# A planner that orders a hybrid trunk's work: a longer visit of small work, and key transposes that come with those of the first queries

## The chip, the cores and the metric

The kernel runs on one core of one Trainium2 chip. The metric is the device time of one execution in microseconds (us). Of the kernel before there are three timed runs, and one further execution under the hardware profiler, from which all rows of the profile come.

## The reference

The reference is a decoder trunk of two residual layers for one sequence of 256 tokens and 1024 channels, in float32. Each layer norms its input, projects it with one wide matrix, feeds three causal mixers in parallel, projects each of them, merges them by sigmoid gates, and projects once more:

```
for layer in range(2):
    h = rms_norm(x, norm_w[layer])
    (a_xbc, a_z, a_dt, b_q, b_k, b_v, b_z, c_q, c_k, c_v, c_f, c_z, gates) = split(h @ w_in[layer])
    y_a = mamba2_branch(a_xbc, a_z, a_dt, ...)           # conv of 4 taps, SiLU, SSD scan, gate, grouped norm
    y_b = sliding_window_branch(b_q, b_k, b_v, b_z, sinks[layer], cos, sin)
    y_c = forgetting_attention_branch(c_q, c_k, c_v, c_f, c_z, ...)
    branch = einsum('bsiw,iwd->bsid', stack(y_a, y_b, y_c), w_proj[layer])
    merged = sum(sigmoid(gates + gate_bias[layer]) * branch)
    x = x + merged @ w_out[layer]
return rms_norm(x, final_norm_w)
```

The sliding branch is what the change is about. It has 16 query heads and 4 key heads of 64 channels. Queries and keys are turned by the rope; each block of 128 queries sees its own and the preceding block of 128 keys under a band mask; a sink per head takes part in the softmax; the result is multiplied by SiLU of b_z.

## The kernel before

**Dense work.** All projections are matmuls in fp32r with weights and inputs split into a high and a low part (hi, lo), in three passes: hi·hi, lo·hi, hi·lo. One dense op is 24 matmuls of 256 or 512 columns into one of three PSUM banks (tiles called mm). A weight tile comes raw from memory (load_to, L368, on SP's queue, which handles its DMAs strictly in order; 6 raw buffers), and ScalarE makes hi (L289) and VectorE lo (L290), 6 buffers each. A unit function (u_bkv, u_bq, u_conv, u_z, u_cv and so on) issues one dense op, then what empties its bank, and then calls pump(). Ops of 512 columns also call it in their middle.

**Small work.** Transposes, scores, softmax, values and the SSD groups are generators that put themselves on a list called waiting by launch(branch, generator, delay), and again with the delay that they yield. A clock that the planner keeps for itself advances with every TensorE instruction that is written out. pump() enters the generator that has been due longest, if one is due and its condition holds, and goes on to the next as long as this visit has used less than BUDGET of the planner's clock:

```
def pump(budget=BUDGET):
    t0 = clock["t"]
    while clock["t"] - t0 < budget:
        for m in sorted(waiting, key=lambda m: (m[0], m[1])):
            if ready(m):
                enter(m)
                break
        else:
            return
```

TensorE runs precisely in this written order. The order on VectorE, ScalarE, GpSimd and SP behind the start is set by a scheduler from the same program, each engine then taking its instructions in order.

**Sliding keys.** u_bkv computes keys and values of one token block (t = 0 or 1), turns the keys by the rope (POOL adds the parts at L529) and launches rest with the delay D_K. rest transposes the keys (L101, to PSUM tiles mx), copies them to kT (L540, ScalarE), and for t = 1, four clock units later, issues two DMAs on SP (L544, 64 partitions each) that write each half of kT to the other half of the partitions. Only then may the scores start.

**Sliding queries.** u_bq does the same with the queries; its rest has the delay D_Q = 5.5, copies at L566 to a tile qt, and for t = 1 launches swa_quad for four heads. swa_quad has three visits to TensorE: 16 scores of a 64-row key tile against qt (mm by L97 into mx); then, behind the softmax (VectorE L671, L674, L681, L684, L686 and L689; ScalarE exp L678 and L683), 8 transposes of pp, which ScalarE copies (L701, L702) and POOL masks (L703, L705); then 16 values, whose product with the gate VectorE takes (L720). A token named pp lets only one quad at a time be between its scores and its values. There are four quads in a layer.

**Between the quads** run the convolutions of the SSD branch: u_conv empties its bank with L799 and L800 on ScalarE, applies three taps on VectorE (L803), a tanh on ScalarE (L806) and a product (L807); u_z makes gates (L863, L866); u_cv makes values of the third branch. The cumulative sums go through memory (cumd: L786 out, L818 and L941 back, on ScalarE's queue). Constants such as the norm's vector (vr, L284) also come on ScalarE's queue.

Of the kernel before, what the change touches and what calls it, by code (L numbers as in the profile page):

```python
# [22 lines left out]
EPS = 1e-6  # L23

D_SOFT, D_EVAC, D_SSD, D_SSD2 = 9.0, 3.0, 8.0, 3.0
D_K, D_Q, D_QK, D_G0, D_FOX, D_BDMA, D_BIAS = 6.0, 5.5, 2.0, 8.0, 0.0, 4.0, 2.0
D_SEL, D_CONST, D_NWB = 5.0, 1.5, 10.0
D_GN1, D_GN2, D_CUM, D_H, D_M = 6.5, 2.5, 12.0, (4.8, 7.0), 5.0
BUDGET = 1.35
T_PP, T_SSD, T_BIAS = 1, 1, 1  # L30
N_RAW, N_SPLIT = 6, 6
AHEAD = 4
# [12 lines left out]
def hybrid_trunk(  # L45
# [83 lines left out]
# [10 lines that stand above are left out]
# [1235 lines left out]
```

## Time and profile before

| what | value |
|---|---|
| three timed runs | 827.72, 828.05, 830.84 us (median 828.05) |
| the profiled execution | 828.2 us, of which the span of all recorded instructions is 826.5 us |
| granted TensorE clock, mean | 0.997 |
| DMA | 158.39 MB, mean 192 GB/s over the span |
| layer 0's sliding quads, conv and SSD | about 50 to 131 us of the span |
| the same of layer 1 | about 455 to 536 us |

PE is TensorE, PEld its loading of weights, DVE VectorE, ACT ScalarE, POOL GpSimd, SP the engine that issues most DMAs. An instruction's row in the timeline has its start, its duration, engine, line, operation, output and inputs by the program's names, and the count when like rows are put together (then the duration goes from the first start to the last end). Matmuls overlap, so starts tell more than durations. In square brackets stands how long the engine was idle before, and what ended that.

### The profile page before, as it was taken

What the parts mean: (1) busy time and instruction counts of PE and PEld (TensorE: products, weight loads), DVE (VectorE), ACT (ScalarE), POOL (GpSimd) and SP (SyncE); (2) the same over time, 40 slices, a digit from 0 to 9 for tenths busy, and PEclk for the clock granted to TensorE, in tenths of its full rate; (3) what the DMA queues carried; (4) which work ended last, traced back from release to release, by engine and by line L of the source; (5) the groups of instructions that cost most, each with busy time, mean ns of one, the idle gap of its engine ahead of it and who ended that gap; (6) DMA issues with size and microseconds to landing.
All of it is one profiled execution on the core that took longest, in us unless ns stands there. A gap on an engine that the chain in (4) does not pass through costs nothing.

```text
span 826.5 us, 15576 instructions
## 1 busy us (share of the span) xinstructions
PE 816.6 (99%) x5777; PEld 743.7 (90%) x5777; DVE 653.8 (79%) x1333; ACT 499.2 (60%) x974; POOL 91.6 (11%) x151
## 2 busy tenths in 40 slices
PE   8999999999999999999999999999999999999996
PEld 7899898988999998888999988898899999988896
DVE  7787998999666788875786879989986667878665
ACT  6476687646666675543664757775556667645442
POOL 3210301000111102100014011100001110021000
PEclk9999999999999999999999999999999999999998
DMA  8945555665765656775687464456676665576632
GB/s 293 287 148 172 178 179 192 181 213 184 213 173 157 215 177 192 225 230 182 213 262 235 135 221 140 138 186 206 190 240 180 178 180 167 162 232 218 217 105 74
DMA packets 124174, 158.39 MB, mean 192 GB/s; under 512 B 12850, under 2 KB 85026, under 8 KB 124099
## 3 DMA queue, kind: packets, MB, share of 16 engines
q1 hardware_dynamic: 109888, 140.92, 55.9%
q10 hardware_dynamic: 14162, 16.36, 6.5%
q8 instruction: 45, 0.74, 0.4%
q14 instruction: 31, 0.25, 0.1%
q0 software_dynamic: 48, 0.13, 0.0%
HBM read 154.70 MB, written 2.16 MB: 190 GB/s over the span
## 4 chain that ended last, share of the span: by engine, by line
PE 94%; DVE 2%; DMA 1%; issue 1%; ACT 1%; ACTq 0%; POOLq 0%; POOL 0%
PE mm L97 79%; PE mx L97 11%; PE mx L101 4%; DMA cumd<-L 1%; DVE lo L290 1%; DVE pp L671 1%; DVE pp L689 0%; DVE L L803 0%; DVE pp L674 0%; ACT L L800 0%; DVE L L866 0%; ACT L L784 0%; ACT L L863 0%; ACT L L799 0%; ACTq L818 0%
## 5 line engine op out<-in xcount | busy, mean ns | idle before, releaser
L290 DVE TENSOR_TENSOR lo<-raw,hi 128x1024 fp32r<-128x1024 f32 x252 | 307.2, 1232 | 64.1 <-ACT hi L289 61.2
L97 PE MATMUL mm<-hi,L 128*128 128x512 f32 (+1 forms) x1264 | 347.7, 363 | 0.9 <-ACT L L800 0.9
L97 PE MATMUL mm<-L,hi 128*128 128x256 f32 x1792 | 310.4, 277 | 0.0
L289 ACT ACTIVATE hi<-raw 128x1024 fp32r<-128x1024 f32 x252 | 261.1, 1054 | 68.7 <-PE mm L97 66.6
L97 PEld LDWEIGHTS mm<-L,hi 128*128 128x128 f32 x1792 | 275.4, 192 | 5.2 <-issue 3.7
L97 PEld LDWEIGHTS mm<-hi,L 128*128 128x128 f32 x1264 | 226.4, 189 | 29.8 <-issue 2.5
L97 PE MATMUL mm<-L,lo 128*128 128x256 f32 x896 | 246.4, 275 | 0.0
L97 PE MATMUL mm<-lo,L 128*128 128x512 f32 (+1 forms) x632 | 224.4, 360 | 0.0
L97 PEld LDWEIGHTS mm<-L,lo 128*128 128x128 f32 x896 | 172.0, 192 | 0.2
L97 PEld LDWEIGHTS mm<-lo,L 128*128 128x128 f32 x632 | 118.8, 189 | 13.7
L948 POOL TENSOR_SCALAR_AFFINE_SELECT bias<-bias 128x128 f32<-128x128 f32 x64 | 24.7, 419 | 290.3 <-DMA bias<-cumd 290.3
L803 DVE SCALAR_TENSOR_TENSOR L<-L,vec,L 128x255 f32<-128x255 f32 (+2 forms) x96 | 47.1, 491 | 4.4 <-ACT L L800 3.1
L972 ACT ACTIVATE L<-L 128x512 f32<-128x512 f32 x24 | 15.1, 630 | 43.0 <-DVE L L971 43.0
L806 ACT ACTIVATE L<-L 128x256 f32<-128x256 f32 x32 | 13.5, 421 | 45.3 <-DVE L L803 45.3
L605 ACT ACTIVATE pp<-pp,nm 128x128 f32<-128x128 f32 x64 | 28.2, 445 | 14.2 <-DVE nm L599 14.2
L97 PE MATMUL mx<-L,L 128*64 128x128 f32 (+1 forms) x384 | 36.5, 332 | 0.0
L97 PEld LDWEIGHTS mx<-L,L 128*64 128x64 f32 x384 | 23.8, 136 | 11.7 <-issue 1.7
L678 ACT ACTIVATE pp<-pp,nm 128x128 f32<-128x128 f32 x64 | 25.3, 395 | 11.7 <-DVE nm L671 6.6
L863 ACT ACTIVATE L<-mm 128x256 f32<-128x256 f32 x48 | 18.1, 376 | 23.0 <-PE mm L97 22.7
L671 DVE CUSTOM_DVE_ANT_0 pp<-mx,wmask,nsink 128x128 f32<-128x128 f32 x64 | 24.3, 412 | 6.0 <-PE mx L97 6.0
L866 DVE SCALAR_TENSOR_TENSOR L<-L,mm 128x256 f32<-128x256 f32 x32 | 13.3, 416 | 16.2 <-ACT L L863 16.2
L97 PE MATMUL mx<-hi,L 128*128 128x512 f32 (+1 forms) x80 | 21.7, 363 | 0.3 <-ACT L L1270 0.2
(184 smaller groups left out, 783.4 us busy)
## 6 DMA issues: line engine op xcount, KB each, us to landing
raw<-in_w_in_dram SPq DMA_DIRECT2D x200, 512.0 KB, 4.6
raw<-in_w_proj_dram SPq DMA_DIRECT2D x48, 512.0 KB, 4.8
raw<-in_w_out_dram SPq DMA_DIRECT2D x16, 512.0 KB, 4.6
L<-cumd ACTq DMA_DIRECT2D x8, 512.0 KB, 3.6
bias<-cumd ACTq DMA_DIRECT2D x16, 256.0 KB, 3.8
L<-in_gate_bias_dram ACTq DMA_DIRECT2D x12, 256.0 KB, 4.2
L<-in_x_dram SPq DMA_DIRECT2D x2, 512.0 KB, 4.0
out_dram<-L SPq DMA_DIRECT2D x2, 320.0 KB, 2.5
```

Source lines behind the costliest of these rows:

```text
L97: nc.tensor.matmul(o, a, b, **kw)
L101: nc.tensor.transpose(o, a, i)
L289: keep(act)(hi, src, AF.Copy)
L290: keep(tt)(lo, src, hi.bitcast(F32), op=ALU.subtract)
L605: act(pp[:, i, sl], pp[:, i, sl], AF.Exp, scale=-1.0, bias=nm[:, e:e + 1], accum_out=sums[:, e:e + 1])
L671: nc.vector.tensor_tensor_reduce(out=pp[:, i, sl], in0=score(p, i, b), in1=m, scale=-0.125, scalar=ns[:, i:i + 1], op0=ALU.add, op1=ALU.mi ...
L678: act(pp[:, i, sl], pp[:, i, sl], AF.Exp, scale=-1.0, bias=nm[:, e:e + 1], accum_out=sums[:, e:e + 1])
L803: stt(a[:, s:S], x_[:, 0:S - s], y.vec[:, 16 * j + u:16 * j + u + 1], a[:, s:S], op0=ALU.mult, op1=ALU.add)
L806: act(th, a, AF.Tanh)
L863: act(halves(th), p, AF.Tanh, scale=0.5)
L948: nc.gpsimd.affine_select(out=bias[:, i, dst], in_=bias[:, i, src], compare_op=ALU.is_ge, fill=NEG, base=0, pattern=[[-1, P]], channel_mul ...
L972: act(g, g, AF.Tanh, scale=0.5)
```

## The change

Two numbers of the planner are changed, and nothing else:

```
-D_K, D_Q, D_QK, D_G0, D_FOX, D_BDMA, D_BIAS = 6.0, 5.5, 2.0, 8.0, 0.0, 4.0, 2.0
+D_K, D_Q, D_QK, D_G0, D_FOX, D_BDMA, D_BIAS = 14.0, 5.5, 2.0, 8.0, 0.0, 4.0, 2.0
...
-BUDGET = 1.35
+BUDGET = 2.0
```

With D_K the keys' transposes are due 14 clock units after the rope instead of 6. With BUDGET a visit that has used 1.35 to 2.0 units may still enter another generator. The number of instructions stays the same on each engine. What the two do to the order shows at three places.

On TensorE, layer 0, where the first sliding quad's values end (mx_1033 is their output, L_56_289 holds kT and the values, qt the second quad's queries, mm_1043 and mm_1093 are the same dense op of u_z, 24 matmuls; numbers of tiles shift between the programs):

```order
 L97 MATMUL mx_1033<-L_202_948,L_56_289 64x256 x2
 L97 MATMUL mx_1033<-L_198_932,L_56_289 64x128 x2
-L97 MATMUL mm_1043<-L_24_147,hi_877 128x256
-L97 MATMUL mm_1043<-L_24_147,lo_878 128x256
-L97 MATMUL mm_1043<-L_25_148,hi_877 128x256
...
+L97 MATMUL mx_1047<-L_56_289,qt_421 128x128
+L97 MATMUL mx_1048<-L_56_289,qt_421 128x128
...
+L97 MATMUL mm_1093<-L_24_147,hi_877 128x256
+L97 MATMUL mm_1093<-L_24_147,lo_878 128x256
+L97 MATMUL mm_1093<-L_25_148,hi_877 128x256
```

The second quad's scores follow the values directly, and the dense op that stood between comes behind them. Layer 1 has the same at the same place. From there to about the fourth quad the small visits of the quads come one dense op, or half of one of 512 columns, earlier than before.

On ScalarE, layer 0, the rows behind the second quad's exponentials, before:

```order
L678 ACTIVATE pp_1084,sums_1086<-pp_1084,nm_1085 128x128 x3
L799 ACTIVATE L_241_1160<-mm_1133 128x256
L678 ACTIVATE pp_1084,sums_1086<-pp_1084,nm_1085 128x128
L683 ACTIVATE es_1126<-es_1126 128x4
L800 ACTIVATE L_240_1159<-mm_1133,vec_647 128x256
L289 ACTIVATE hi_1264<-raw_970 128x1024
L289 ACTIVATE hi_1282<-raw_988 128x1024
```

and now, of the same engine from the same exponentials on:

```order
L678 ACTIVATE pp_1044,sums_1046<-pp_1044,nm_1045 128x128 x4
L683 ACTIVATE es_1086<-es_1086 128x4
L863 ACTIVATE L_237_1130<-mm_1093 128x256
L289 ACTIVATE hi_1182<-raw_881 128x1024
L289 ACTIVATE hi_1200<-raw_899 128x1024
L818 DMA L_439_2214<-cumd_1031 128x1024
L799 ACTIVATE L_241_1160<-mm_1133 128x256
L800 ACTIVATE L_240_1159<-mm_1133,vec_647 128x256
```

The exponentials of the second quad (pp) have moved ahead of the first convolution's bank copies (mm_1133, L799 and L800), and no longer mix with them.

On SP, layer 0, the weight loads and the two DMAs of kT (L544; one row stands for both):

```order
-L368 DMA raw_451<-in_w_in_dram 128x4x256
-L368 DMA raw_463<-in_w_in_dram 128x4x256
-L544 DMA L_56_289<-L_56_289 64x2x256 x2
+L368 DMA raw_441<-in_w_in_dram 128x4x256
+L368 DMA raw_453<-in_w_in_dram 128x4x256
+L368 DMA raw_466<-in_w_in_dram 128x4x256
 L368 DMA raw_478<-in_w_in_dram 128x4x256
-L368 DMA raw_490<-in_w_in_dram 128x4x256
 L368 DMA raw_576<-in_w_in_dram 128x4x256
 L368 DMA raw_582<-in_w_in_dram 128x4x256
+L544 DMA L_56_289<-L_56_289 64x2x256 x2
```

The kT DMAs stand behind four more weight loads than before (raw_478, raw_490, raw_576 and raw_582 by the names before); in layer 1 they also stand behind four more. The keys' transposes on TensorE come, for layer 0, in one visit with the first queries', and for the second token block of layer 1 with queries of the same block, one dense op behind where those stood.

## The prediction

> **What bounds the kernel now.** I read the page first, then the list of TensorE's waits, then the two places where that list says time is lost, then the queues that the change moves. From the page:
>
> ```profile
> span 826.5 us, 15576 instructions
> PE 816.6 (99%) x5777; PEld 743.7 (90%) x5777; DVE 653.8 (79%) x1333; ACT 499.2 (60%) x974; POOL 91.6 (11%) x151
> PEclk9999999999999999999999999999999999999998
> PE 94%; DVE 2%; DMA 1%; issue 1%; ACT 1%; ACTq 0%; POOLq 0%; POOL 0%
> ```
>
> TensorE is busy for 99% of the span, at a full granted clock, and 94% of the chain that ends last is its work. So a change of order can only move time in two ways: it takes away or adds a wait of TensorE, or it changes what TensorE pays between two kinds of matmul. All waits that the view of TensorE's waits lists (total, times, longest, in us):
>
> ```profile
> PE mx L101 <- POOL ident masks.py:199: 1.5, 1, 1.5
> PE mm L97 <- ACT L L800: 0.9, 2, 0.5
> PE mx L97 <- ACT L L1270: 0.2, 1, 0.2
> PE mx L101 <- issue: 0.2, 1, 0.2
> ```
>
> The first is the start of the kernel, which the change leaves alone. Behind it 1.3 us are left, and 0.9 of these are two waits for one thing, a copy by ScalarE at L800. They are the only ones within the stretches that the change orders anew. Since no more than that is there to be won, a gain of over 4 us has no place to come from. The measurement of this kernel can tell about 0.5% (4 us) from no change.
>
> The timeline of TensorE shows these two waits (start, duration, x count). The first two rows are a visit of the same kind that does not wait; the next two are layer 0's, the last two layer 1's:
>
> ```profile
> 107.86 1.04 PE L101 MATMUL mx<-ident,pp 128*128 128x128 f32 x8
> 108.66 0.36 PE L97 MATMUL mm<-L,hi 128*128 128x256 f32 x1
> ...
> 87.39 1.04 PE L101 MATMUL mx<-ident,pp 128*128 128x128 f32 x8
> 88.88 0.70 PE L97 MATMUL mm<-hi,L 128*128 128x512 f32 x2 [0.45 <-ACT L L800]
> ...
> 492.21 1.04 PE L101 MATMUL mx<-ident,pp 128*128 128x128 f32 x8
> 493.74 0.70 PE L97 MATMUL mm<-hi,L 128*128 128x512 f32 x2 [0.49 <-ACT L L800]
> ```
>
> Undisturbed, eight transposes take 0.80 us from their first start to the next dense matmul (107.86 to 108.66). Here it is 1.49 and 1.53: 0.69 + 0.73 = 1.42 us lost. (The bracket says 0.45 and 0.49, because a busy matmul's end is modelled; I go by starts.) The cause stands in ScalarE's and VectorE's timelines of layer 0:
>
> ```profile
> 83.45 1.05 ACT L289 ACTIVATE hi<-raw 128x1024 fp32r<-128x1024 f32 x1
> 87.69 0.42 ACT L806 ACTIVATE L<-L 128x256 f32<-128x256 f32 x1 [3.18 <-DVE L L803]
> 88.01 0.36 ACT L799 ACTIVATE L<-mm 128x256 f32<-128x256 f32 x1
> 88.27 0.56 ACT L800 ACTIVATE L<-mm,vec 128x256 f32<-128x256 f32 x1
> ...
> 84.98 0.69 DVE L689 TENSOR_TENSOR pp<-pp,rsum 128x512 f32<-128x512 f32 x1
> 87.11 0.48 DVE L803 SCALAR_TENSOR_TENSOR L<-L,vec,L 128x253 f32<-128x253 f32 x1
> ```
>
> ScalarE stands 3.18 us in front of the tanh of one convolution (L806). That waits for the last tap on VectorE (L803, 87.11), which stood behind the softmax of the second quad (L689, 84.98). Behind the tanh in ScalarE's queue are L799 and L800 of the next convolution, which empty a PSUM bank; TensorE's next op in that bank starts 0.05 us after L800's 0.56 us are over (88.27 + 0.56 = 88.83; 88.88).
>
> **The change part by part.** *The visit that lasts longer.* In each layer, at one place, the scores of the second quad now follow the values of the first; before, one dense op of 24 matmuls of 256 columns stood between. The matmuls are the same, so what is saved is what TensorE pays between kinds. The rows of the separate visits, and of one visit that was merged already:
>
> ```profile
> 71.22 1.04 PE L97 MATMUL mx<-L,L 128*64 128x128 f32 x12
> 72.19 0.38 PE L97 MATMUL mm<-L,hi 128*128 128x256 f32 x1
> 72.40 0.28 PE L97 MATMUL mm<-L,lo 128*128 128x256 f32 x1
> 72.51 0.28 PE L97 MATMUL mm<-L,hi 128*128 128x256 f32 x1
> ...
> 74.86 0.28 PE L97 MATMUL mm<-L,hi 128*128 128x256 f32 x1
> 75.06 0.93 PE L97 MATMUL mx<-L,qt 64*128 64x128 f32 x8
> ...
> 94.74 1.04 PE L97 MATMUL mx<-L,L 128*64 128x128 f32 x12
> 95.71 0.93 PE L97 MATMUL mx<-L,qt 64*128 64x128 f32 x8
> ```
>
> Twelve values take 0.97 us to the start of what follows, be it dense work (71.22 to 72.19) or scores (94.74 to 95.71). But the first dense matmul then holds its successor for 0.21 (72.19 to 72.40) where 0.11 is the rule (72.40 to 72.51), and the last one before scores takes 0.20 (74.86 to 75.06). Merged, both extras go: 0.10 + 0.09 = 0.19 us a place, two places, **−0.4 us**. [...]
>
> *What follows from it.* The softmax of the second quad starts one dense op (24 x 0.11 = 2.7 us) earlier, and its transposes come earlier too. On ScalarE its exponentials now stand ahead of L799/L800 of the first convolutions instead of among them, and on VectorE its last product (84.98) comes about 2.7 us earlier, at 82.3, ahead of the taps. Then the tap of 87.11 is over near 84.9, tanh and the next convolution's L799/L800 by 86.2 (0.42 + 0.36 + 0.56), and TensorE wants the bank at 88.0 (87.39 + 0.80 less the 0.2 of the merged visit): 1.8 us to spare. **−1.4 us** for the two stalls. What is late next: the values of the same quad wait for GpSimd's mask of the exponentials' transposes, as they do now:
>
> ```profile
> 94.11 0.58 POOL L705 TENSOR_SCALAR_AFFINE_SELECT L<-L 128x256 f32<-128x256 f32 x1
> ```
>
> The mask ends at 94.69, 0.05 us ahead of values at 94.74. Everything in that chain of visits moves by the same step, so I take no new wait; if ScalarE's copies ahead of the mask are late by as much as an L289 (1.05 us in the rows above), each layer loses up to 1.0 us.
>
> *The keys' transposes.* The same transposes, copies (L540) and DMAs (L544) come later. A visit of transposes costs TensorE no extra beyond the 0.08 us of one slow successor (108.66's row), so merging with the queries' saves at most 0.1 us a time: 0. What can cost is the landing of the L544 DMAs ahead of the first scores. Layer 1, where it is tightest; the timeline rows of TensorE, ScalarE and SP, and the source view of L544:
>
> ```profile
> 443.67 0.60 PE L101 MATMUL mx<-ident,L 128*128 128x128 f32 x4
> 454.84 0.93 PE L97 MATMUL mx<-L,qt 64*128 64x128 f32 x8
> ...
> 438.46 0.78 ACT L540 ACTIVATE L<-mx 64x256 f32<-64x256 f32 x2 [4.40 <-PE mx L101]
> 438.87 1.29 SPq L544 DMA_DIRECT2D L<-L  x2
> 446.56 0.37 SPq L368 DMA_DIRECT2D raw<-in_w_in_dram  x1
> 450.80 0.37 SPq L368 DMA_DIRECT2D raw<-in_w_in_dram  x1
> ...
> DMA to landing us min/median/max: 2.7/5.0/7.4
> ```
>
> In the new order the transposes stand one dense op behind the place at 443.67, about 446.3. Six transposes (0.7) and two pairs of copies (2 x 0.78) bring it to about 448.4. The DMAs stand on SP behind four more weight loads, of which the last issued at 446.56 before, so SP is free: issues at 448.4 and 449.0. Landing at 451.7 by the shortest row, 454.0 by the median, 456.4 by the longest, against scores at 454.84. I take the short one, since both layer-1 rows are of this place: 3 us to spare, **0 us**; the far end is +1.6 us. Behind them on SP waits the load of 450.80, which isn't reached. In layer 0 the DMAs go from 27.2 to about 36, and the scores start at 50: 36 + 7.4 leaves 6 us.
>
> One DMA that the diff does not name moves with them. In layer 0 the load of the norm's vector on ScalarE's queue now waits for the landing of a weight that SP issues near 32.2:
>
> ```profile
> 32.23 2.92 SPq L368 DMA_DIRECT2D raw<-in_w_in_dram  x3
> ...
> 45.42 0.24 PE L101 MATMUL mx<-ident,vr 88*128 88x88 f32 x1
> ...
> DMA to landing us min/median/max: 3.1/5.4/12.2
> ```
>
> With 7.4 us for that weight (the longest L544 above, issued in the same stretch) it issues at 39.6, and with its own line's median of 5.4 (last row) lands at 45.0, against its transpose at 45.42. I take +0.1 us; with the longest, 12.2, it would be +6.4.
>
> **The sum** is made against the profiled execution, 828.2 us (span 826.5 and 1.7 around it), 0.15 above the median of the three runs shown (828.05). 828.2 − 0.4 − 1.4 + 0 + 0.1 = 826.5. Set against the median it is 826.3; I say 826.4.
>
> **The rivals.** *The stalls change place.* Another of the engines' queues holds the bank, or the mask is late: −0.4 remains and about as much is lost elsewhere (1.4 us, up to 2.0 with the mask in both layers): 827.8 to 828.4. For it: a bank goes back only 0.05 us ahead of its use today, and masks likewise. Against: by the starts above there are 1.8 us in hand. 0.20.
>
> *Slower: the key copies are late in layer 1.* The last weight load in front of them comes free one step later, at 450.80 and not 446.56; then they issue at 451.2 and 451.8 and land at 454.5, 456.8 or 459.2. It decides from a landing after 454.84: 0, +2.0 or +4.4 us, with a gain of 1.7 beside it: 826.5 to 830.9, likeliest 828.5 where it bites. For it: the buffers of raw weights set those times, and the order of their readers shifts. Against: nothing else was moved there. 0.08. The clock: the PEclk row is full throughout, and no wait of TensorE in it exceeds 1.5 us. [...] 0.01.
>
> *Slower: the norm vector is late in layer 0.* It decides from a landing time of 5.8 us (45.42 − 39.6), close to the median of 5.4; at 12.2 it costs 6.4: 826.4 to 832.8. For it: four weight loads are in flight at that time. Against: few rows are that long. 0.08.
>
> **How the numbers follow.** Forecast 0.57 (826.4; by its bounds 825.6 to 828), stalls elsewhere 0.20, keys late 0.08, clock 0.01, norm vector 0.08, a wait that I don't see in the reordered stretch 0.05 (up to 8 us), a gain that I don't see 0.01. Faster by over 0.5% (under 823.9) only by the last: 0.02 with the spread of runs. Slower by over 0.5% (over 832.2): the unseen wait, the upper end of the norm vector and the clock, 0.05 + 0.02 + 0.01 = 0.08. The rest, 0.90, is within. The range goes from 825.5 to 830.9, the upper end of the keys' case.
>
> **What would show it.** Right: no row with a wait for L800 near 86 to 89 and 490 to 494; the second quad's scores right behind the first's values, near 72 us; all waits behind the start under 0.6 us in sum. Wrong: a wait of the 64*128 scores for a DMA near 455, of the 88x88 transpose for a DMA near 45, of values for L705, or again for L800. A span 4 us away from 825 would mean that a wait was missed, or that TensorE's busy time is not the same for the same matmuls.

## The result and the profile after

The changed kernel takes 836.83 us (median of 6 runs, 834.47 to 838.27); the kernel before, over the runs taken beside it and earlier, 829.2 us (827.26 to 830.84). The ratio is 1.0094, with a 95% interval of 1.0079 to 1.011: slower by 0.9%, where 0.2% faster was forecast. The profiled execution takes 836.13 us, with a span of 834.0. Its page:

```profile
span 834.0 us, 15592 instructions
PE 820.0 (98%) x5777; PEld 745.7 (89%) x5777; DVE 654.7 (78%) x1333; ACT 500.5 (60%) x974; POOL 92.1 (11%) x151
...
PEclk9999899999999999999999999999999999999999
...
PE 91%; issue 6%; POOL 2%; ACT 0%; DVE 0%; POOLq 0%
```

The work is the same; the chain now has POOL in it, and the clock row has an 8 in its fifth slice. (The 6% of issue are two pieces of 22 us, one in each layer, in which the chain runs through POOL's idle time ahead of L948.) The view of TensorE's waits (total, times, longest):

```profile
PE mx L97 <- POOL L L703: 3.1, 3, 1.3
PE mx L97 <- POOL L L705: 2.3, 3, 1.2
PE mx L101 <- POOL ident masks.py:199: 1.5, 1, 1.5
PE mm L97 <- ACT L L1270: 0.2, 1, 0.2
```

The two waits for L800 are gone, as forecast. In their place stand 5.4 us of waits for the masks of the second sliding quad. POOL's timeline of layer 0, the kernel before:

```profile
87.18 1.53 POOL L948 TENSOR_SCALAR_AFFINE_SELECT bias<-bias 128x128 f32<-128x128 f32 x4 [20.84 <-DMA bias<-cumd]
89.35 2.38 POOL L948 TENSOR_SCALAR_AFFINE_SELECT bias<-bias 128x128 f32<-128x128 f32 x4 [0.64 <-DMA bias<-cumd]
91.69 1.38 POOL L703 TENSOR_SCALAR_AFFINE_SELECT L<-L 128x256 f32<-128x256 f32 x1
```

and the changed one:

```profile
88.64 2.77 POOL L948 TENSOR_SCALAR_AFFINE_SELECT bias<-bias 128x128 f32<-128x128 f32 x4 [22.44 <-DMA bias<-cumd]
91.36 0.58 POOL L703 TENSOR_SCALAR_AFFINE_SELECT L<-L 128x256 f32<-128x256 f32 x1
91.90 1.39 POOL L705 TENSOR_SCALAR_AFFINE_SELECT L<-L 128x256 f32<-128x256 f32 x1
93.24 0.58 POOL L703 TENSOR_SCALAR_AFFINE_SELECT L<-L 128x256 f32<-128x256 f32 x1
93.78 1.22 POOL L948 TENSOR_SCALAR_AFFINE_SELECT bias<-bias 128x128 f32<-128x128 f32 x4
94.97 0.41 POOL L705 TENSOR_SCALAR_AFFINE_SELECT L<-L 128x256 f32<-128x256 f32 x1
```

L948 makes the causal masks of the third branch's bias tiles, which are read back from memory (L941). They belong to work much later, but POOL takes them in its queue's order when they land. Before, both tiles stood ahead of the quad's masks. Now the transposes come 3 us earlier (84.38 instead of 87.39), the first tile still stands ahead of the masks, and the second tile stands between the third mask and the fourth. TensorE's timeline shows what that costs; first the changed kernel's layer 0, then its layer 1:

```profile
90.31 0.38 PE L97 MATMUL mm<-lo,L 128*128 128x512 f32 x1
92.00 0.65 PE L97 MATMUL mx<-L,L 128*64 128x256 f32 x4 [1.31 <-POOL L L703]
93.34 1.66 PE L97 MATMUL mx<-L,L 128*64 128x128 f32 x8 [0.69 <-POOL L L705]
95.42 0.69 PE L97 MATMUL mx<-L,L 128*64 128x128 f32 x4 [0.42 <-POOL L L705]
96.05 2.93 PE L97 MATMUL mx<-L,qt 64*128 64x128 f32 x16
98.91 1.22 PE L97 MATMUL mm<-hi,L 128*128 128x512 f32 x2
...
500.17 0.38 PE L97 MATMUL mm<-lo,L 128*128 128x512 f32 x1
...
505.54 1.58 PE L97 MATMUL mx<-L,qt 64*128 64x128 f32 x16
507.05 0.70 PE L97 MATMUL mm<-hi,L 128*128 128x512 f32 x2
```

From the last dense matmul to the next one it takes 8.60 us in layer 0 and 6.88 in layer 1. The same visit without a wait takes 3.28 (it is in the run a_late below, 93.12 to 96.40). So 5.3 and 3.6 us are lost. In layer 0 part of this is the clock, because TensorE runs at half speed there (granted clock 0.50 from 94 to 100 us): from the first score to the next dense matmul it takes 2.86 us (96.05 to 98.91) instead of the 1.51 of a_late (94.89 to 96.40). Behind the visit another 0.6 us go the same way: the next five dense matmuls take 1.80 us (98.91 to 100.71) instead of the 1.18 of layer 1 (507.05 to 508.23). The windows view has the granted clock as the number behind POOL's busy time and count:

```profile
90.00:92.00 2.00, 0.69 (x4) 0.26 (x3) 2.00 (x4) 1.67 (x4) 2.00 (x4) 1.00 0.15 54
92.00:94.00 2.00, 1.31 (x10) 0.61 (x12) 1.97 (x3) 0.00 (x0) 2.00 (x3) 0.84 0.80 217
94.00:96.00 2.00, 1.58 (x10) 0.47 (x8) 0.10 (x1) 0.00 (x0) 1.37 (x5) 0.50 0.87 261
96.00:98.00 2.00, 2.00 (x16) 1.78 (x16) 1.35 (x3) 0.42 (x1) 0.00 (x0) 0.50 0.13 50
98.00:100.00 2.00, 2.00 (x9) 1.17 (x8) 2.00 (x13) 1.38 (x6) 0.00 (x0) 0.50 0.01 4
100.00:102.00 2.00, 2.00 (x10) 1.77 (x9) 2.00 (x13) 1.83 (x9) 0.00 (x0) 0.95 0.00 0
```

The account closes: 5.3 + 0.6 + 3.6 lost, 1.4 (L800) and 0.4 (the merged visits) won, 7.7 in all; from the first dense matmul to the end the two profiles differ by 819.97 − 812.35 = 7.6 us.

### The profile page after: what moved, and what is told of

The parts are those of the page before. It is cut to its first block, busy times and chain, and to the rows that moved or that the text cites. A ratio compares the mean times of both kernels' runs of the same rounds, so it can differ in the third digit from the quotient of the medians.

```text
span 834.0 us, 15592 instructions
## 1 busy us (share of the span) xinstructions
PE 820.0 (98%) x5777; PEld 745.7 (89%) x5777; DVE 654.7 (78%) x1333; ACT 500.5 (60%) x974; POOL 92.1 (11%) x151
## 4 chain that ended last, share of the span: by engine, by line
PE 91%; issue 6%; POOL 2%; ACT 0%; DVE 0%; POOLq 0%
PE mm L97 77%; PE mx L97 10%; PE mx L101 4%; POOL bias L948 1%; POOL L L703 1%; POOL L L705 0%; ACT L L701 0%; ACT L L1110 0%; ACT L L1270 0%; POOLq L1370 0%; ACT L L226 0%; DVE L L1090 0%; POOL ident masks.py:199 0%; POOLq L948 0%; DVE sm L239 0%
## 5 line engine op out<-in xcount | busy, mean ns | idle before, releaser
L290 DVE TENSOR_TENSOR lo<-raw,hi 128x1024 fp32r<-128x1024 f32 x252 | 307.8, 1234 | 67.4 <-ACT hi L289 61.9
L289 ACT ACTIVATE hi<-raw 128x1024 fp32r<-128x1024 f32 x252 | 261.7, 1054 | 61.2 <-PE mm L97 58.5
L948 POOL TENSOR_SCALAR_AFFINE_SELECT bias<-bias 128x128 f32<-128x128 f32 x64 | 25.1, 425 | 300.7 <-DMA bias<-cumd 172.3
L97 PE MATMUL mx<-L,L 128*64 128x128 f32 (+1 forms) x384 | 38.5, 340 | 5.4 <-POOL L L703 3.1
```

Of the source, the lines that this page charges most:

```text
L97: nc.tensor.matmul(o, a, b, **kw)
L289: keep(act)(hi, src, AF.Copy)
L290: keep(tt)(lo, src, hi.bitcast(F32), op=ALU.subtract)
L948: nc.gpsimd.affine_select(out=bias[:, i, dst], in_=bias[:, i, src], compare_op=ALU.is_ge, fill=NEG, base=0, pattern=[[-1, P]], channel_mul ...
```

## The experiments

**How they are compared.** The start of the kernel takes one of two lengths, and the times of the kernel before fall into two groups 2.5 to 3 us apart. TensorE's timelines show it at the first dense matmul, here of before (828.2 us) and of dk_only (830.82 us):

```profile
14.15 0.75 PE L97 MATMUL mm<-hi,L 128*128 128x256 f32 x4
...
16.94 0.73 PE L97 MATMUL mm<-hi,L 128*128 128x256 f32 x4 [0.22 <-ACT L L1270]
```

For a single profile the table therefore also has the time from there to the span's end, in which the start does not count. It is one execution each, and the span is read to 0.1 us; the ratios with their intervals come from the timed runs, each against runs of before taken beside it. The medians of those were 829.2 for changed, 828.53 for dk_only, budget_only, a_late and b_late, 828.81 for a_late2, warm and a_late_soft, and 830.43 for a_dma and a_dma_soft, so ratios compare and medians do not.

| kernel | median us (runs) | ratio to before (95%) | first dense matmul to end, us |
|---|---|---|---|
| before | see above | 1 | 812.35 |
| changed | 836.83 (6) | 1.0094 (1.0079 to 1.011) | 819.97 |
| dk_only | 828.27 (10) | 0.9997 (0.9982 to 1.0011) | 812.16 |
| budget_only | 835.89 (4) | 1.0082 (1.0061 to 1.0104) | 819.76 |
| b_late | 830.3 (12) | 1.0007 (0.9993 to 1.0022) | 812.33 |
| a_late | 828.9 (12) | 0.9995 (0.998 to 1.0009) | 811.56 |
| a_late2 | 830.1 (10) | 1.0015 (0.9999 to 1.0031) | 811.37 |
| warm | 836.17 (4) | 1.0081 (1.0062 to 1.01) | 817.91 |
| a_dma | 830.52 (10) | 1.002 (1.0005 to 1.0035) | 814.26 |
| a_dma_soft | 830.17 (12) | 1.0021 (1.0007 to 1.0034) | 814.28 |
| a_late_soft | 826.31 (12) | 0.9971 (0.9958 to 0.9983) | 810.46 |

**dk_only and budget_only: which of the two numbers.** `D_K = 14.0` alone, and `BUDGET = 2.0` alone, each in the kernel before.

> The kernel before with D_K = 14 alone (BUDGET stays 1.35). Theory POOL (the loss comes from the second quad's masks L703/L705, which wait in POOL's queue behind bias masks L948 that wait for a DMA; it comes from BUDGET alone): 828 to 829.5 us, ratio to before 0.998 to 1.002, POOL's order as before, and the two waits for L800 still there. Rival KEYS (the later key copies or the weight loads they stand among cost it): 832 to 837 us, with waits of TensorE near 45 or 455 us.

> The kernel before with BUDGET = 2.0 alone (D_K stays 6). Theory POOL: 835 to 838 us, ratio 1.008 to 1.011, with 5 to 6 us of waits of TensorE for L703 and L705 in the two layers. Rival KEYS: 826 to 829 us. A half clock behind the waits of a layer (as in layer 0 of the changed kernel) may or may not show; if it does only in some layers, the clock and not only the waits decides 2 to 3 us.

D_K alone changes nothing that can be measured (0.9997; 0.2 us in the profile), and no row of it has a wait near 45 or 455 us. BUDGET alone is the whole loss. Its waits view, and POOL's timeline of layer 0:

```profile
PE mx L97 <- POOL L L705: 5.3, 3, 2.8
```

```profile
89.05 0.59 POOL L703 TENSOR_SCALAR_AFFINE_SELECT L<-L 128x256 f32<-128x256 f32 x1
91.20 2.60 POOL L948 TENSOR_SCALAR_AFFINE_SELECT bias<-bias 128x128 f32<-128x128 f32 x4 [1.56 <-DMA bias<-cumd]
93.76 0.67 POOL L705 TENSOR_SCALAR_AFFINE_SELECT L<-L 128x256 f32<-128x256 f32 x1
```

Here the mechanism is bare, in layer 0: three masks are over by 89.64, ahead of the values, and only the fourth waits, behind a tile that has not landed (1.56 us of idle POOL) and then takes 2.60 us itself.

**a_late and b_late: the bias masks behind the quad's masks.** One order edge on POOL, in the changed kernel and in the kernel before; TensorE, ScalarE, VectorE and SP keep their order:

```
-                    nc.gpsimd.affine_select(out=bias[:, i, dst], ...)
+                    with tc.issue_after(y.masked[1].ins) if j == 0 else ExitStack():   # last L705 of quad 2
+                        nc.gpsimd.affine_select(out=bias[:, i, dst], ...)
```

> The changed kernel with one order edge: the first fox quad's bias masks (L948 there) stand on POOL behind the second sliding quad's masks. All other engines keep the order of the changed kernel. Theory POOL: the waits for L703 and L705 (5.4 us) and the half clock behind them are gone, and what was forecast blind is left: 826 to 828 us, ratio to before 0.996 to 0.999. Rival EARLY (the visit is simply too early for ScalarE's copies of the transposes, L701 and L702, whatever POOL does): 830 to 834 us, the waits for POOL replaced by waits of about 1 to 2 us a layer that end with L702's masks.

> The kernel before with the same order edge on POOL. Theory POOL: no change, 0.999 to 1.001; the second quad's masks end 2 us ahead of the values instead of 0.05, which shows that the kernel before had the bias masks just hidden; the two waits for L800 remain. Rival EARLY: the same. If it is slower than before by more than 0.2%, the later bias masks themselves cost something that would also stand in the other run.

In a_late the waits for POOL are gone and the visit of values and scores is whole (TensorE's timeline):

```profile
93.12 0.38 PE L97 MATMUL mm<-lo,L 128*128 128x512 f32 x1
93.43 1.52 PE L97 MATMUL mx<-L,L 128*64 128x256 f32 x16
94.89 1.58 PE L97 MATMUL mx<-L,qt 64*128 64x128 f32 x16
96.40 0.70 PE L97 MATMUL mm<-hi,L 128*128 128x512 f32 x2
```

Against the changed kernel that is 8.4 us less in the profile, with no other engine's order changed: POOL's order is the cause, and ScalarE's copies are early enough. Yet the ratio to before is 0.9995 and the profile 0.8 us below it; more than half of the forecast gain is missing. Its waits view says where it is:

```profile
PE mx L101 <- DVE pp L689: 0.8, 2, 0.5
```

Both waits are of the fourth quad's transposes, which wait for the last product of its softmax. Layer 0's starts in a_late:

```profile
126.79 0.60 PE L101 MATMUL mx<-ident,pp 128*128 128x128 f32 x4
127.85 0.63 PE L101 MATMUL mx<-ident,pp 128*128 128x128 f32 x4 [0.46 <-DVE pp L689]
```

Four transposes take 0.44 us by starts (0.11 apart, 84.48, 84.59 and 84.70 in the changed kernel), here 1.06: 0.62 lost, and 0.50 in layer 1. b_late is the same as before within its interval, and 0.02 us off in the profile: the bias masks cost nothing where they stood before, and nothing where the edge puts them. The last mask of the second quad is over 1.28 us ahead of the values that read it (93.73 and 95.01), where the kernel before has 0.70; the 2 us that were expected were not reached.

**a_late2: which bias tile.** The edge for the second tile's four masks alone.

> The changed kernel with only the second tile's bias masks (four L948) behind the second sliding quad's masks; the first tile's four stay in front, with their wait for the DMA. If the wait in front (the landing at 88.6 us and 2.8 us of masks) is the larger part: 816.5 to 818.5 us from the first dense matmul, against 819.98, since only the 1.2 and 1.5 us of the second tile's masks in the middle go. If the masks in the middle are the cause: about 812 us.

The expectation that the first tile is the larger part fell. POOL's timeline:

```profile
87.15 1.25 POOL L950 TENSOR_SCALAR_AFFINE_SELECT bias<-bias 128x128 f32<-128x128 f32 x4 [20.95 <-DMA bias<-cumd]
88.36 0.62 POOL L703 TENSOR_SCALAR_AFFINE_SELECT L<-L 128x256 f32<-128x256 f32 x1
...
91.47 2.58 POOL L950 TENSOR_SCALAR_AFFINE_SELECT bias<-bias 128x128 f32<-128x128 f32 x4 [1.06 <-DMA bias<-cumd]
```

The first tile landed at 87.15 in this execution (88.64 in the changed kernel's profile), and its masks were out of the way. The second lands at 91.47, after the values are due. With its masks out of the middle the ratio falls from 1.0094 to 1.0015, so over the timed runs they are the main cause. The first tile is not free either. In the changed kernel's own profile its masks run until 91.41, past the 90.62 at which the values start in a_late2, and the masks in the middle hold the last one back by no more than 1.2 us (93.78 to 94.97). And the ten runs spread from 827.49 to 833.93, wider than a_late's 826.89 to 830.53, as a tile that lands early in some executions and late in others would do. That reading of the spread is argued, since only one execution has a trace.

**warm: the half speed.** In the changed kernel 14 transposes of a constant ahead of each pair of the second quad's values (their results are unused):

```
+        pw = pmx() if c == 1 else None
         for p in range(2):
+            for n in range(14 if c == 1 else 0):
+                nc.tensor.transpose(pw[:, 0:P], ident, ident)
```

> The changed kernel with 28 transposes of a constant (results unused; 3.0 us at full clock) put into TensorE's waits ahead of the second quad's values, 14 ahead of each pair. The waits for POOL end when they did. If the half speed behind them comes from TensorE being too little busy in them, it goes, and with it 2.7 us in layer 0: 816.5 to 818 us from the first dense matmul, granted clock near 1.00 in 51 to 131 us. If the half speed has another cause: 820 us or more, up to 823 where the transposes delay the values, and the clock dips again.

The clock does what was expected: the windows view of layer 0 has it at 1.00 where the changed kernel has 0.81 over the same 18 us.

```profile
84.00:102.00 18.00, 18.00 (x142) 15.95 (x141) 16.44 (x42) 11.46 (x32) 6.48 (x12) 1.00 0.65 207
```

```profile
84.00:102.00 18.00, 15.58 (x92) 11.81 (x92) 14.42 (x42) 10.37 (x31) 6.74 (x12) 0.81 0.54 177
```

The first is warm, the second the changed kernel. From the first dense matmul it is 2.1 us faster, within what was expected, and 2.0 is what the scores and the dense matmuls behind them had paid in layer 0 (1.35 + 0.62); the median of its four timed runs (836.17 against 836.83) does not settle that gain. The masks did not end when they had: the fourth is over 4.0 us behind the start of the last dense matmul in layer 0 and 5.4 in layer 1, against 5.1 and 4.9 in the changed kernel, which nearly cancels. From that matmul to the next dense one it still takes 6.63 and 7.35 us instead of 3.28. So the late masks remain the cause, and the clock is a consequence: in a_late, without them and without these transposes, it is at 1.00 over 84 to 102 us too.

**a_dma and a_dma_soft: the bias DMAs early.** Another cure: the two DMAs (L941) in a `with tc.high_priority():`, so that they stand right behind the cumulative sums on ScalarE's queue; a_dma_soft adds the delay of the next experiment.

> The changed kernel with the two bias DMAs (L941) of a fox quad issued on ScalarE's queue as early as they can be, that is right behind the cumulative sums' way out. On POOL all eight bias masks stand in front of the second quad's masks. If the masks' cost is the wait for the bias DMAs' landing, as the last experiment suggests: the bias masks are over near 83 us, before the second quad's masks come, no wait for L703 or L705 is left, and 811.3 to 812 us from the first dense matmul, times 0.997 to 1.000 of before. If POOL has simply too many masks ahead: 815 us or more, with waits for L703 or L705.

> The same with the fourth quad's transposes half a dense op later, as in a_late_soft. Theory: as a_late_soft, 810.3 to 810.8 us from the first dense matmul, times 0.9960 to 0.9985 of before, since the two cures of POOL are worth the same. If the early DMAs slow ScalarE (they stand in front of the second quad's exponentials and wait for cumd), 811 us or more.

For the masks it holds. POOL makes all eight bias masks at 78.31, ahead of the quad, and no wait for L703 or L705 is left:

```profile
78.31 5.01 POOL L949 TENSOR_SCALAR_AFFINE_SELECT bias<-bias 128x128 f32<-128x128 f32 x8 [12.11 <-DMA bias<-cumd]
```

So it is the landing and not the number of masks ahead that counts. But the times missed their forecasts, a_dma's by 2.3 us or more and a_dma_soft's by 3.5 or more. The orders on ScalarE and VectorE changed as well, and now the third quad's transposes wait for its softmax, in both runs by the same amount:

```profile
PE mx L101 <- DVE pp L689: 3.4, 2, 1.8
```

Without these 3.4 us both would stand near 810.9 by this sum. Which of the moved instructions makes the softmax late was not tested.

**a_late_soft: the version that beats both.** a_late, and the fourth quad's transposes half a dense op later:

```
-        yield D_SOFT
+        yield D_SOFT + (1.5 if c == 3 else 0.0)
```

> The changed kernel with the bias masks behind the second quad's masks, as in a_late, and the fourth quad's transposes half a dense op later (1.5 clock units more behind its softmax). All times here from the first dense matmul to the span's end, since the start takes one of two lengths: before 812.35, changed 819.98, a_late 811.56 us in their profiles. Theory: a_late lost 0.62 + 0.50 us of the forecast gain to transposes that wait for the softmax's last product (L689) at 127 and 531 us; half an op later this wait goes: 810.3 to 810.8 us, ratio of times to before 0.996 to 0.999. Rival: the wait moves to the fourth quad's values, or to the SSD groups behind it: 811.4 us or more.

826.31 us, ratio 0.9971 (0.9958 to 0.9983): faster than the kernel before by 0.3%, and from the first dense matmul to the end 9.5 us less than the changed one. The waits view has nothing left in the two stages of the quads:

```profile
PE mx L101 <- POOL ident masks.py:199: 1.5, 1, 1.5
PE mm L97 <- ACT L L1272: 0.2, 1, 0.2
```

## Why the prediction was wrong

- **What bounds it: right.** TensorE's work is the same, and the whole difference is in waits and in the clock behind them. But "a gain of over 4 us has no place to come from" bounds a gain alone. For a loss the prediction allowed 1.0 us a layer, by the row of an L289 on ScalarE, which is not what made the masks late.
- **The merged visit (−0.4) and the stalls of L800 (−1.4): right.** No wait for L800 is left in the changed kernel. In a_late_soft, where the new waits are taken away, 812.35 − 810.46 = 1.9 us are won from the first dense matmul on; the sum of the two terms was 1.8.
- **"Everything in that chain of visits moves by the same step, so I take no new wait": this step failed.** The masks' inputs came earlier, but the masks stand in a queue with L948, whose tiles land when their DMA does. The second tile's DMA even issued later (it starts at 84.50 instead of 82.66, where it took 1.85 us), because ScalarE's queue had been reordered too. The prediction quoted the mask that ends at 94.69 and did not ask what kept it until then: the rows above it in the same timeline were L948 with a DMA as their releaser. The new orders of TensorE, ScalarE and SP were read, POOL's was not, though L948 between L703 and L705 stands in it. It was this queue that decided.
- **"0.05 us ahead of values at 94.74": misread.** The row at 94.74 is the rest of a visit that starts at 94.26. The four values that read the last mask (the ones that wait for L705 at 95.42 in the changed kernel) start later in the kernel before, so the slack was 0.70 us:

```profile
95.39 0.39 PE L97 MATMUL mx<-L,L 128*64 128x128 f32 x4
```

- **The rival "the stalls change place" had the place and not the size.** It allowed 1.0 us a layer for a late mask, from one L289 on ScalarE. Measured: 5.9 us in layer 0 and 3.6 in layer 1.
- **The clock: underrated.** It had a case of its own (0.01), against which stood that no wait before exceeds 1.5 us; no run shows the loss by which this case counts among the times over 832.2. In the changed kernel the granted clock fell to 0.50 in layer 0 with no gap over 1.31 us, and cost 2.0 of the 5.9 us there.
- **The keys' transposes (0) and the norm vector (+0.1): right, as far as a term of 0.1 can be told.** dk_only is at 0.9997, and no wait for a DMA stands near 455 or 45 us in it or in the changed kernel.
- **Not seen: the fourth quad.** a_late's wait for L689 (1.1 us in two layers) was in no term or rival; by itself it leaves a gain of 0.7 instead of 1.8 even with POOL in order, and a_late's profile has 0.8.

## What to carry to other kernels

Where a step is moved earlier, each of its inputs moves only as far as the queue that makes it: read the new order on every engine that touches the step, the little used ones above all, and look for instructions there that wait for a DMA. A row that ends just ahead of its reader needs one more look at what started it; if that is a landing and not the chain that was moved, the slack is already spent. And where a planner counts TensorE's time alone, a cheap order edge on the side engine can take such a loss away (a_late); here the gain that was meant took one more delay (a_late_soft).

## What the runs showed of the hardware

**The clock.** It fell to half in layer 0 of the changed kernel (1.00 from 90 to 92 us, 0.84 from 92 to 94, 0.50 from 94 to 100) after some 3 us in which TensorE was partly busy (0.69 of 90 to 92 us, 1.31 of 92 to 94), and did not in layer 1, where the waits were of the same kind (1.07, 1.10 and 0.84 us busy in the three stretches from 500 to 506 us, granted clock 1.00); in budget_only it showed 0.91 over 84 to 102 us and again over 490 to 510. The longest gap of the changed kernel was 1.31 us in layer 0 (ahead of 92.00) and 1.16 in layer 1 (ahead of 505.17); why the clock fell in the one layer and not in the other, no run shows. In warm, with unused transposes in the gaps, the granted clock was 1.00 over 84 to 102 and over 490 to 510 us; that is one execution.

**POOL beside VectorE.** In the changed kernel a mask of POOL took 0.40 us with VectorE idle (L705 at 504.71, VectorE idle from 504.10 to 505.65), and up to 1.39 us beside L290, the subtraction of two tiles in SBUF (L705 at 91.90, L290 from 91.60 to 93.02; that mask ends at 93.29, 0.27 us behind L290); the eight L948 of layer 0 took 2.77 and 1.22 us for four each. No run here was made to test whether L290 is what makes the mask longer.
